# Two parts of every weight tile made by GpSimd DMAs (a casting load, a negation, an accumulating load) in place of a raw tile, ScalarE and VectorE

## The chip, the cores and the metric

The kernel runs on one core of one Trainium2 chip. The metric is device time in microseconds (us), first to last instruction of the program. Engines are PE (TensorE matmul), PEld (its weight load), DVE (VectorE), ACT (ScalarE), POOL (GpSimd) and SP (SyncE, which only issues DMAs here). Each works through its own list of instructions in order, and waits on semaphores for the others.

## The reference

A token sequence of 512 with 1024 features goes through two blocks. Block 1 is a mixer of four branches (Mamba-2, RG-LRU, retention, RWKV-7) and a feed-forward part; block 2 has two layers, each with three kinds of attention, a feed-forward part and a per-layer embedding. Nearly all arithmetic is in products of a normalised activation with a weight matrix, all in float32:

```python
def hybrid_mixer(h, w_in, ssm_p, lru_p, ret_p, rwkv_p, w_branch, w_out, cos, sin):
    proj = h @ w_in
    ...
    branch = jnp.einsum('bsmw,mwd->bsmd', ys, w_branch)
    ...
    return merged @ w_out

def conv_ffn(h, w_up, conv_w, conv_b, w_down):
    u = causal_dwconv(h @ w_up, conv_w, conv_b)
    val, gt = jnp.split(u, 2, axis=-1)
    return (jax.nn.silu(gt) * val) @ w_down
```

## The kernel before, in words

Activations stand with features on the 128 partitions and the 512 tokens along a row. To multiply float32 numbers at the fast rate, each operand is split in two parts that are exact in the rounded format F32R: `hi` is the operand rounded, `lo` is the operand minus `hi`. A product is three matmuls: hi by hi, lo by hi and hi by lo (`mm3`).

Weights come in tiles of 128 partitions by up to 1024 columns (512 KB), one tile for 128 output features and 1024 input features. `wtile` makes the two parts of one: SP loads the raw tile `wr` (3 buffers, `NWR`), ACT copies it rounded into `whi` (3 buffers), DVE writes the difference into `wlo` (2 buffers). A tile of 1024 columns then feeds 24 matmuls of 512 columns into one PSUM tile `pj`; a tile of 512 columns feeds 12, one of 256 columns 6. 579 such tiles go through the kernel. The third matmul of a tile is the first one that reads `wlo`.

A scheduler orders each engine's list when the program is built; the lists are fixed then. A tile's buffer is handed to the tile that comes as many tiles later as the pool has buffers, when the last matmul that reads it has ended. So `whi` of tile k can be written when PE has finished tile k-3, and `wlo` when PE has finished tile k-2.

Three places matter below. The feed-forward stretches (`ffn`, 1250 to 1640, 2250 to 2600 and 3280 to 3650 us) are 1024-column tiles back to back (768 columns at the end of each). In `attn_a_setup` (about 1640 to 1700 and 2640 to 2700 us) every projection tile alternates with a tile of `cmp_w1` that feeds only 8 matmuls of 256 columns. In `branch2` (to about 2160 and 3160 us) tiles of 512 columns of `w_br2` follow one another. POOL had little to do: zeroing of tiles, and the power -1/2 of each norm (`rsqrt`, the tiles `r`, `ors`, `rrs`).

Of the kernel before, what the change touches and what calls it, by code (L numbers as in the profile page):

```python
# [10 lines left out]
F32 = mybir.dt.float32  # L11
F32R = mybir.dt.float32r
I32 = mybir.dt.int32
AF = mybir.ActivationFunctionType
ALU = mybir.AluOpType
# [12 lines left out]
NWR = 3  # L28
# [10 lines left out]
def _param_layout():  # L39
    """Columns of the packed per-feature parameters: name -> (first column, columns)."""  # L40
# [17 lines left out]
# constants that depend on shapes alone: name -> (first column, columns)  # L58
# [15 lines left out]
class Unit:  # L74
    """Softmax attention of 128 queries over T sets of n keys that share a bank of scores."""
# [65 lines left out]
class B:  # L141
    """The parts of the program share these helpers, pools and constants."""
# [66 lines left out]
    def split(self, hi, lo, src, scale=None):  # L209
        """hi + lo == src (times a per-feature column), each part exact in the fast format."""  # L210
        if scale is None:
            self.act(hi, src, AF.Copy)
            self.tt(lo, src, hi.bitcast(F32), ALU.subtract)
        else:
            self.act(hi, src, AF.Copy, scale=scale)
            self.stt(lo, src, scale, hi.bitcast(F32), ALU.mult, ALU.subtract)

    def wtile(self, src, n=1024):
        raw = self.wr.tile([P, 1024], F32, tag="wr", name=self.name("wr"))
        self.dma(raw[:, :n], src)  # L220
        hi = self.wh.tile([P, 1024], F32R, tag="whi", name=self.name("whi"))
        lo = self.wh.tile([P, 1024], F32R, tag="wlo", name=self.name("wlo"), bufs=2)
        self.split(hi[:, :n], lo[:, :n], raw[:, :n])
        return hi, lo

    def mm3(self, out, ws, xs, first, last):
        """out += (wh + wl)^T (xh + xl) without the product of the two low parts."""
# [5 lines left out]
    def pmm(self, w, off, x, kc, m=P):  # L233
        """One chunk of m output features from the split weights w, from column off on."""
# [7 lines left out]
    def proj(self, src, x, kc=KC, m=P):  # L242
        """One chunk of m output features: src is [128, kc * m] of DRAM, x the split activations."""
        return self.pmm(self.wtile(src, kc * m), 0, x, kc, m)

    def rsqrt(self, out, ss, scale, eps):
        """out = (ss * scale + eps) ** -0.5 on a few columns."""
# [5 lines left out]
    def col_sums(self, out, xs):  # L253
        """out[:, t]: sums of the columns of all xs, tokens on partitions."""
# [6 lines left out]
    def rstd_rows(self, sq, dst, n=D):  # L261
        """sq: [128, S] (or several), whose column sums are sums of squares; dst[:, t] = rsqrt(mean + eps)."""
# [6 lines left out]
    def bcast_cols(self, r, dst):  # L269
        """The columns r [128, 4] of tokens as one row [., S] on every partition."""  # L270
# [9 lines left out]
    def softplus_neg_abs(self, out, ax, tmp):  # L280
        """out = log1p(exp(-ax)) for ax >= 0, by 2 atanh(e / (2 + e))."""
# [24 lines left out]
    def block1_consts(self):  # L306
# [23 lines left out]
        # 4 * softplus(-lam)  # L330
# [14 lines left out]
    def first_norm(self):  # L345
        """h = rms_norm(x) in two parts, features on partitions."""
# [28 lines left out]
    # -- RWKV --  # L375
    def rwkv_setup(self, pool):
# [11 lines left out]
        # w2: high parts on the lower half of the partitions, low parts on the upper; a2 the other way round  # L388
# [12 lines left out]
    def mix(self, pool, ps, ch, tag, bufs):  # L401
        """Token shift: x (1 - mu) + previous x mu."""
# [5 lines left out]
    def rwkv_lora(self, pool):  # L408
        """Chunks 24 (wl | al) and 25 (gl) of the mixed projection."""
# [20 lines left out]
    def lora(self, i, cs):  # L430
        """The second product of decay (0) or rate (1): (high + low) high, then high low."""
# [13 lines left out]
    def rwkv_core(self, pool, p):  # L445
# [6 lines left out]
        # decay  # L452
# [11 lines left out]
        # a  # L464
# [5 lines left out]
        # normalised key direction  # L470
# [19 lines left out]
        # bonus  # L490
# [6 lines left out]
        # values, tokens of a chunk on partitions, the two heads stacked  # L497
# [57 lines left out]
    def swap_halves(self, dst, src):  # L555
        """dst[(h, t), c, v] = src[(h, v), (c, t)] for halves h of the partitions and chunks c of 64."""
# [9 lines left out]
    def rwkv_inverse(self, pool):  # L566
        """(I + A)^-1 of every head and chunk, A strictly upper triangular: forward substitution in the two
        diagonal blocks of 32, one problem a partition, then the block above them by matrix products."""
# [25 lines left out]
        # four problems on the partitions: -X11 (A12 X22), with A12 and then (X11 A12)^T on block diagonals  # L594
# [60 lines left out]
    def rwkv_step(self, pool, p, c, st, ld, bank):  # L655
        """One chunk of the recurrence over the states of a pair of heads."""
# [32 lines left out]
    def rwkv_scan(self, pool, p, y):  # L689
        """The recurrence of a pair of heads, its norm and output."""  # L690
# [38 lines left out]
    # -- RG-LRU --  # L729
    def conv4(self, pool, ps, w, n, ch, b, tag, bufs=2, taps=4):  # L730
        """Causal depthwise convolution along the tokens of [128, S]."""
# [47 lines left out]
    # -- Mamba-2 --  # L779
    def silu_gate(self, pool, ps, tag, tmp, bufs=1):  # L780
        """silu(ps) = (1 + tanh(x / 2)) x / 2."""
# [7 lines left out]
    def ssm_setup(self, pool, tmp):  # L789
        """dt, its cumulative sums about each block's middle, and what follows from them."""  # L790
# [38 lines left out]
        # from the block's start, and about its middle  # L829
# [7 lines left out]
        # dt exp(end - cum)  # L837
# [112 lines left out]
    # -- retention --  # L950
    def rope(self, pool, ps, cos, sin, half, rows, tag, bufs=1, tmp=(("ropr", 1), ("rops", 1))):
        """x cos + swap(x) sin, halves of each head swapped across partitions by DMA."""
# [12 lines left out]
    def stack(self, pool, src, e, tag, bufs=1):  # L965
        """[high; low] parts of head e stacked on the partitions."""
# [6 lines left out]
    def dup(self, pool, src, e, tag, bufs=1):  # L973
        """The high part of head e on both halves of the partitions, and the low part."""
# [9 lines left out]
    def ret_pair(self, pool, j, y):  # L984
# [7 lines left out]
        # values with tokens on partitions  # L992
# [54 lines left out]
    def finish_ret(self):  # L1047
        """The last steps of the heads whose norms were begun one stage before."""
# [8 lines left out]
    # -- gates, branch products, merge --  # L1057
# [4 lines left out]
    def gates1(self, pool):  # L1062
        """tanh(gate / 2) of the four branches, chunk by chunk."""
# [7 lines left out]
    def branch(self, pool, m, y, gates, norm=None):  # L1071
        """merged (+)= (1 + tanh(gate / 2)) * (y_m W_m): twice the gated sum."""
# [20 lines left out]
    def norm_in(self, pool, c, x, w, acc, tag="nsq", bufs=2, gain=1.0):  # L1093
        """Chunk c of x (times gain) joins the sum of squares; its product with w is split into h."""
# [11 lines left out]
    def new_row(self):  # L1106
        """The row of 1 / rms by which products with h are still to be multiplied."""
# [6 lines left out]
    def out_proj(self, pool, w, m, xres, gain, g0, tag="xr", bufs=4, due=None):  # L1114
        """x += m w; the new x goes to DRAM, its normalised form to h. due: a row and gains still missing in x."""
# [15 lines left out]
    def ffn(self, up, down, conv, pool, done, mid=None, late=None):  # L1131
        """x + W_down (silu(gate) value); done(j, x_j) takes each finished chunk."""
# [51 lines left out]
    def embeddings(self, pool, i, tags=None):  # L1184
        """The per-layer embeddings p W of layer i, to DRAM."""
# [22 lines left out]
    def mid_norm(self, pool, fill):  # L1208
        """Block 1's last norm and block 2's first: x still lacks the first one's gain and row1, h the row of both."""
# [19 lines left out]
    def block1(self):  # L1229
# [10 lines left out]
        def weave(main, fill, ratio):  # L1240
            """One step of `fill` after every `ratio` steps of `main`; then what is left of fill."""
# [99 lines left out]
    def rope_tables(self, tmp):  # L1341
        """cos and signed sin of positions x frequencies, the angle reduced to [-pi, pi]."""
# [38 lines left out]
    def rope_load(self, pool, n, row):  # L1381
        """The rotary tables, times the row of 1 / rms if that is still due."""
# [18 lines left out]
    def rope2(self, pool, pt, cs, half, tag="ra", bufs=2):  # L1401
        """x cos + swap(x) sin, halves of each head swapped across partitions by DMA."""
# [16 lines left out]
    def to_tokens(self, pool, src, tag, rows=P, n=P, bufs=1):  # L1419
        """[rows, S] features x tokens to [128 tokens, 4, n]."""  # L1420
# [8 lines left out]
    def compress(self, pool, i, src, kv, out):  # L1429
        """gelu((blocks + pos) w1): leaves the hidden activations' transpose [128, 2, 64] in out."""  # L1430
# [15 lines left out]
        for t in range(4):  # L1446
            # high parts in columns 0 to 63 of each product's stationary operand, low parts in the others
# [659 lines left out]
```

## Time and profile before

| What | Value |
|---|---|
| Median of 3 runs | 3707.62 us (3706.73 to 3713.56) |
| Profiled execution, its own time as the span from first to last instruction | 3707.9 us |
| PE busy | 3630.3 us (98%) |
| DVE busy | 2328.7 us (63%) |
| ACT busy | 1543.6 us (42%) |
| POOL busy | 53.2 us (1%) |
| DMA queue q1 | 414.84 MB, 36.3% of 16 engines |

The profiled execution lies within 0.3 us of the median, so its rows can be added up against either. A share of busy time is a mean over stages; PE's 98% leaves 77.6 us in which it stood idle.

### The profile page before, as it was taken

What the parts mean: (1) busy time and instruction counts of PE and PEld (TensorE: products, weight loads), DVE (VectorE), ACT (ScalarE), POOL (GpSimd) and SP (SyncE); (2) the same over time, 40 slices, a digit from 0 to 9 for tenths busy, and PEclk for the clock granted to TensorE, in tenths of its full rate; (3) what the DMA queues carried; (4) which work ended last, traced back from release to release, by engine and by line L of the source; (5) the groups of instructions that cost most, each with busy time, mean ns of one, the idle gap of its engine ahead of it and who ended that gap; (6) DMA issues with size and microseconds to landing.
All of it is one profiled execution on the core that took longest, in us unless ns stands there. A gap on an engine that the chain in (4) does not pass through costs nothing.

```text
span 3707.9 us, 47402 instructions
## 1 busy us (share of the span) xinstructions
PE 3630.3 (98%) x17806; PEld 2953.0 (80%) x17806; DVE 2328.7 (63%) x4416; ACT 1543.6 (42%) x2619; POOL 53.2 (1%) x61
## 2 busy tenths in 40 slices
PE   8999999999999999999999999999999999999998
PEld 6887788877878788877888787888778887878886
DVE  6777897654454586657776655544677766554445
ACT  5665533323233353344555533222445655432223
POOL 0000000000000000000000000000000000000000
PEclk9999999999999999999999899999999999999999
DMA  5443545355543532344222124233442221343332
GB/s 182 141 135 116 154 123 142 107 152 161 158 132 108 162 108 91 103 135 150 76 66 68 58 82 154 92 96 95 139 134 80 64 69 55 102 141 96 95 93 97
DMA packets 230388, 417.86 MB, mean 113 GB/s; under 512 B 99632, under 2 KB 105648, under 8 KB 230032
## 3 DMA queue, kind: packets, MB, share of 16 engines
q1 hardware_dynamic: 230160, 414.84, 36.3%
q8 instruction: 141, 2.31, 0.3%
q14 instruction: 87, 0.71, 0.1%
HBM read 349.81 MB, written 55.38 MB: 109 GB/s over the span
## 4 chain that ended last, share of the span: by engine, by line
PE 66%; DVE 2%; ACT 1%; issue 0%; DMA 0%; POOL 0%; SPq 0%; POOLq 0%; DVEq 0%; ACTq 0%
PE pj L173 56%; PE ps L173 4%; PE pl L173 4%; PE ps L119 2%; DVE wlo L176 0%; DVE cc L176 0%; PE ps L1589 0%; POOL r L251 0%; ACT PT L166 0%; DVE ro L176 0%; ACT qf L166 0%; ACT P L167 0%; DVE kd L176 0%; DVE qf L176 0%; DVE xa L193 0%
## 5 line engine op out<-in xcount | busy, mean ns | idle before, releaser
L173 PE MATMUL pj<-hhi,whi 128*128 128x512 f32 (+1 forms) x2824 | 1137.6, 403 | 6.4 <-DVE scv L193 2.1
L173 PE MATMUL pj<-hhi,wlo 128*128 128x512 f32 (+1 forms) x2824 | 1127.2, 399 | 5.9 <-DVE wlo L176 5.8
L173 PE MATMUL pj<-hlo,whi 128*128 128x512 f32 (+1 forms) x2824 | 1128.0, 399 | 0.0
L166 ACT ACTIVATE whi<-wr 128x1024 fp32r<-128x1024 f32 (+3 forms) x579 | 573.4, 990 | 1289.1 <-PE pj L173 1140.3
L176 DVE TENSOR_TENSOR wlo<-wr,whi 128x1024 fp32r<-128x1024 f32 (+3 forms) x579 | 654.8, 1131 | 165.1 <-PE pj L173 104.2
L173 PEld LDWEIGHTS pj<-hhi,wlo 128*128 128x128 f32 (+1 forms) x2824 | 531.4, 188 | 135.9 <-DVE wlo L176 10.3
L173 PEld LDWEIGHTS pj<-hhi,whi 128*128 128x128 f32 (+1 forms) x2824 | 532.1, 188 | 130.8 <-issue 3.3
L173 PEld LDWEIGHTS pj<-hlo,whi 128*128 128x128 f32 (+1 forms) x2824 | 532.2, 188 | 122.8 <-issue 4.5
L173 PE MATMUL pj<-gl,whi 128*128 128x512 f32 x528 | 208.6, 395 | 0.0
L173 PE MATMUL pj<-gh,wlo 128*128 128x512 f32 x528 | 208.6, 395 | 0.0
L173 PE MATMUL pj<-gh,whi 128*128 128x512 f32 x528 | 208.5, 395 | 0.0
L176 DVE TENSOR_TENSOR fg<-pj,row 128x512 f32<-128x512 f32 x82 | 56.7, 691 | 212.7 <-PE pj L173 212.6
L176 DVE TENSOR_TENSOR xa<-pj,xa 128x512 f32<-128x512 f32 x72 | 49.8, 692 | 193.5 <-PE pj L173 193.3
L167 ACT ACTIVATE P<-ps,a 128x256 f32<-128x256 f32 (+3 forms) x256 | 128.3, 504 | 53.8 <-DVE a L189 49.9
L173 PE MATMUL pj<-o,whi 128*128 128x512 f32 x384 | 132.5, 421 | 0.0
L173 PE MATMUL pj<-yh,whi 128*128 128x512 f32 x320 | 131.1, 410 | 1.4 <-ACT yh L166 1.4
L173 PE MATMUL pj<-yl,whi 128*128 128x512 f32 x320 | 129.4, 404 | 0.5 <-DVE yl L176 0.5
L173 PE MATMUL pj<-yh,wlo 128*128 128x512 f32 x320 | 128.9, 403 | 0.0
L166 ACT ACTIVATE PT<-ps 128x256 f32<-128x256 f32 (+3 forms) x200 | 98.3, 492 | 71.0 <-PE ps L119 56.9
L173 PEld LDWEIGHTS pj<-gl,whi 128*128 128x128 f32 x528 | 99.0, 187 | 24.3
L173 PEld LDWEIGHTS pj<-gh,whi 128*128 128x128 f32 x528 | 99.0, 187 | 24.2
L173 PEld LDWEIGHTS pj<-gh,wlo 128*128 128x128 f32 x528 | 99.0, 187 | 24.2
(504 smaller groups left out, 5209.9 us busy)
## 6 DMA issues: line engine op xcount, KB each, us to landing
wr<-in_ffn_up SPq DMA_DIRECT2D x132, 512.0 KB, 3.4
wr<-in_w_in SPq DMA_DIRECT2D x122, 512.0 KB, 3.7
wr<-in_ffn_down SPq DMA_DIRECT2D x48, 512.0 KB, 3.5
wr<-in_w_bg SPq DMA_DIRECT2D x48, 512.0 KB, 3.4
wr<-in_w_gate SPq DMA_DIRECT2D x32, 512.0 KB, 3.5
wr<-in_w_branch SPq DMA_DIRECT2D x32, 512.0 KB, 3.5
wr<-in_w_out SPq DMA_DIRECT2D x24, 512.0 KB, 3.5
wr<-in_w_br SPq DMA_DIRECT2D x48, 256.0 KB, 2.6
```

The source lines that it names most:

```text
L119: b.nc.tensor.transpose(pt[:, k * P:(k + 1) * P], self.P[:, k * P:(k + 1) * P], b.ident)
L166: return self.nc.scalar.activation(out, in_, f, bias=bias, scale=scale)
L167: return self.nc.scalar.activation(out, in_, f, bias=bias, scale=scale, accum_out=accum)
L173: return self.nc.tensor.matmul(out, lhsT, rhs, start=start, stop=stop)
L176: return self.nc.vector.tensor_tensor(out, a, b, op=op)
```

## The change

`wtile` loses the raw tile. POOL issues a DMA that casts the weights from DRAM into `whi`, ACT writes the negative of `whi` into `wlo`, and POOL issues a second DMA of the same weights that adds to `wlo`. `whi` has 4 buffers in place of 3, `wlo` 3 in place of 2; the raw pool keeps one buffer for the two low-rank weight tiles that still use it. DVE no longer takes part, and SP no longer loads weights through `wtile`. The file also loses its comments, so that line numbers move by one to three.

```diff
-NWR = 3
+NWR = 1
+NWT = 4
...
     def wtile(self, src, n=1024):
-        raw = self.wr.tile([P, 1024], F32, tag="wr", name=self.name("wr"))
-        self.dma(raw[:, :n], src)
-        hi = self.wh.tile([P, 1024], F32R, tag="whi", name=self.name("whi"))
-        lo = self.wh.tile([P, 1024], F32R, tag="wlo", name=self.name("wlo"), bufs=2)
-        self.split(hi[:, :n], lo[:, :n], raw[:, :n])
+        hi = self.wh.tile([P, 1024], F32R, tag="whi", name=self.name("whi"), bufs=NWT)
+        lo = self.wh.tile([P, 1024], F32R, tag="wlo", name=self.name("wlo"), bufs=NWT - 1)
+        self.nc.gpsimd.dma_start(hi[:, :n], src)
+        self.act(lo[:, :n], hi[:, :n].bitcast(F32), AF.Copy, scale=-1.0)
+        self.nc.gpsimd.dma_start(lo[:, :n], src, accum_op=ALU.add)
         return hi, lo
```

The first place is the feed-forward part of block 2's first layer. On DVE of before, the two `wlo` of a pair of tiles stand between the products that take results out of PSUM (`fv`, `fg` from `pj`):

```order
L176 TENSOR_TENSOR fv4022_19737<-pj4021_19712,row3932_19302 128x512
L176 TENSOR_TENSOR wlo4031_19781<-wr4029_19778,whi4030_19780 128x1024
L176 TENSOR_TENSOR fg4027_19770<-pj4026_19745,row3932_19302 128x512
L176 TENSOR_TENSOR wlo4036_19814<-wr4034_19811,whi4035_19813 128x1024
L193 SCALAR_TENSOR_TENSOR fth4028_19772<-fth4028_19772,fg4027_19770 128x512
L176 TENSOR_TENSOR fth4028_19772<-fth4028_19772,fv4022_19737 128x512
L193 SCALAR_TENSOR_TENSOR gl3960_19343<-fth4028_19772,gh3952_19335 128x512
```

The list of POOL in the changed kernel at the same place has two DMAs a tile, and the cast of a tile stands ahead of the accumulation of the tile before it:

```order
L224 DMA whi3659_19225<-in_ffn_up2 128x1024
L226 DMA wlo3655_19188<-in_ffn_up2 128x1024
L224 DMA whi3663_19257<-in_ffn_up2 128x1024
L226 DMA wlo3660_19226<-in_ffn_up2 128x1024
L224 DMA whi3668_19295<-in_ffn_up2 128x1024
L226 DMA wlo3664_19258<-in_ffn_up2 128x1024
```

The list of ACT there has the negations where `whi` stood before, two to four tiles ahead of the result (`fth`, `gh`) that follows them:

```order
L167 ACTIVATE wlo3655_19188<-whi3654_19187 128x1024
L167 ACTIVATE wlo3660_19226<-whi3659_19225 128x1024
L167 ACTIVATE fth3649_19149<-fg3648_19147 128x512
L167 ACTIVATE gh3617_19000<-fth3649_19149 128x512
L167 ACTIVATE wlo3664_19258<-whi3663_19257 128x1024
L167 ACTIVATE wlo3669_19296<-whi3668_19295 128x1024
```

What moved: the writing of `wlo` from DVE's list to POOL's, with a step on ACT between its two DMAs; on DVE the rows of `wlo` are gone and nothing stands in their place.

The second place is `attn_a_setup` of the first layer, on POOL of the changed kernel (`in_cmp_w1` are the short tiles, `in_w_in2` the projections):

```order
L224 DMA whi2337_13406<-in_cmp_w1 128x1024
L226 DMA wlo2332_13364<-in_w_in2 128x1024
L224 DMA whi2339_13419<-in_w_in2 128x1024
L226 DMA wlo2338_13407<-in_cmp_w1 128x1024
L224 DMA whi2347_13468<-in_cmp_w1 128x1024
L224 DMA whi2349_13481<-in_w_in2 128x1024
L226 DMA wlo2340_13420<-in_w_in2 128x1024
L226 DMA wlo2348_13469<-in_cmp_w1 128x1024
L226 DMA wlo2350_13482<-in_w_in2 128x1024
```

Here two casts stand ahead of three accumulations at one point; on SP of before one load stood for each of these tiles.

The third place is the beginning, on POOL of the changed kernel (`in_w_pp` are the embeddings' weights, `r435` the first norm):

```order
L224 DMA whi25_125<-in_w_pp 128x1024
...
L226 DMA wlo26_126<-in_w_pp 128x1024
L224 DMA whi47_221<-in_w_pp 128x1024
L224 DMA whi57_382<-in_w_in 128x1024
L254 TENSOR_TENSOR r435_167<-rs36_168,mhalf_90 128x4
L224 DMA whi61_422<-in_w_in 128x1024
L226 DMA wlo48_222<-in_w_pp 128x1024
```

The accumulation into the second embedding tile (`wlo48`) now stands behind the first norm's power on POOL's list.

## Rows read from the trace of the kernel before

**Rows 1.** The page: busy us, share, instructions; then the chain that ended last.

```profile
PE 3630.3 (98%) x17806; PEld 2953.0 (80%) x17806; DVE 2328.7 (63%) x4416; ACT 1543.6 (42%) x2619; POOL 53.2 (1%) x61
PE 66%; DVE 2%; ACT 1%; issue 0%; DMA 0%; POOL 0%; SPq 0%; POOLq 0%; DVEq 0%; ACTq 0%
```

**Rows 2.** Waits of PE: for whom, total us, times, longest.

```profile
PE pj L173 <- ACT whi L166: 10.2, 3, 8.6
PE ps L173 <- DVE dg L176: 7.6, 10, 2.1
PE pj L173 <- DVE wlo L176: 5.8, 7, 1.5
...
PE ps L173 <- DVE hl L176: 5.4, 2, 3.6
```

**Rows 3.** Windows, feed-forward stretch: us, PE, PEld, DVE, ACT, POOL busy (instructions), PEclk, DMA share, GB/s.

```profile
3300.00:3400.00 100.00, 100.00 (x430) 80.60 (x429) 50.65 (x63) 29.21 (x36) 0.00 (x0) 1.00 0.30 95
```

**Rows 4.** Weight tiles' instructions in that stretch: duration ns least/median/most, first and last start.

```profile
L166 ACT ACTIVATE whi<-wr x18: 1062/1062/1062, 3299.7 to 3394.9; 128x1024 fp32r<-128x1024 f32 x18
L176 DVE TENSOR_TENSOR wlo<-wr,whi x18: 1218/1218/1218, 3300.5 to 3395.7; 128x1024 fp32r<-128x1024 f32 x18
```

**Rows 5.** DMA issues: count, KB each, median us from issue to landing.

```profile
wr<-in_ffn_up SPq DMA_DIRECT2D x132, 512.0 KB, 3.4
wr<-in_w_in SPq DMA_DIRECT2D x122, 512.0 KB, 3.7
wr<-in_w_pp SPq DMA_DIRECT2D x4, 512.0 KB, 4.5
xt<-in_xT SPq DMA_DIRECT2D x8, 256.0 KB, 6.0
```

**Rows 6.** POOL's instructions by line: count, busy us, mean ns, idle before.

```profile
L251 POOL TENSOR_TENSOR r<-rs,mhalf 128x4 f32<-128x4 f32 x15 | 16.2, 1078 | 2584.1 <-DVE rs L190 2584.1
L600 POOL MEMSET invbd<- 128x2048 f32 x1 | 1.8, 1814 | 57.1 <-DVE invt L176 57.1
```

**Rows 7.** Windows of weight tiles alone: DVE and ACT busy (tiles), PEclk, whole DMA share, GB/s.

```profile
800.00:900.00 100.00, 14.63 (x12) 13.74 (x13) 0.93 0.60 165
1600.00:1700.00 100.00, 21.13 (x20) 19.50 (x20) 0.98 0.51 160
2200.00:2300.00 100.00, 21.83 (x20) 19.27 (x19) 1.00 0.50 163
```

**Rows 8.** Timeline in `attn_a_setup`: start, us, engine, what, [idle before, releaser].

```profile
1677.87 0.50 PE L173 MATMUL pj<-hhi,wlo 128*128 128x512 f32 x1 [0.91 <-DVE wlo L176]
...
1685.03 0.39 PE L173 MATMUL ps<-whi,hl 128*128 128x256 f32 x1 [1.76 <-DVE hl L176]
1685.25 0.28 PE L173 MATMUL ps<-wlo,hl 128*128 128x256 f32 x1
1685.37 0.28 PE L173 MATMUL ps<-whi,hl 128*128 128x256 f32 x1
...
1686.31 0.63 PE L173 MATMUL pj<-hhi,whi 128*128 128x512 f32 x1
1686.74 0.63 PE L173 MATMUL pj<-hlo,whi 128*128 128x512 f32 x1
```

**Rows 9.** Windows: the stretch behind that wait, and the first full-rate loads.

```profile
1685.00:1690.00 5.00, 4.97 (x22) 4.32 (x23) 5.00 (x8) 1.91 (x3) 0.00 (x0) 0.66 0.48 124
8.00:14.00 6.00, 5.33 (x13) 3.79 (x14) 4.65 (x7) 5.05 (x9) 0.00 (x0) 1.00 1.00 385
```

**Rows 10.** Timeline of the beginning.

```profile
0.73 0.20 POOL masks.py:197 MEMSET ident<- 128x128 f32 x1 [0.29 <-POOLq L2098]
...
9.88 0.80 PE L173 MATMUL pj<-ph,wlo 128*128 128x512 f32 x1
...
17.52 1.02 POOL L251 TENSOR_TENSOR r<-rs,mhalf 128x4 f32<-128x4 f32 x1 [16.22 <-DVE rs L190]
...
19.89 0.80 PE L173 MATMUL pj<-ph,whi 128*128 128x512 f32 x1
```

## Prediction

> **What bounds the kernel now.** I read the page's busy line first. PE works 3630.3 of 3707.9 us [rows 1], so it stands idle for 77.6 us in all, and its own 66% is the main part of the chain that ended last. Then I read for whom PE waits. The longest waits are the 8.6 us before the first product, and a handful of 1 to 4 us for DVE; all waits for `wlo` come to 5.8 us [rows 2]. Then the feed-forward stretch: 430 products in 100 us, 0.233 us apart, at a granted clock of 1.00, while DVE is busy for half of the time and the DMA engines for 0.30 of it [rows 3]. 18 weight tiles go through it, one in 5.6 us, each with one copy of 1.06 us on ACT and one difference of 1.22 us on DVE [rows 4]. Nothing but PE is near its limit there.
>
> So the change can win only out of waits that are small already, and loses wherever a weight tile comes late. The question is how long the new way to a weight tile takes, against how early it can begin.
>
> **What is removed.** 579 differences leave DVE, some 655 us of its 2328.7 (1131 ns each as a mean over all sizes). They are hidden behind PE now, and DVE is not the bound, so most of that buys nothing. What it can buy is PE's waits for DVE: with `wlo` and `hl` gone it is 5.8 + 5.4 = 11.2 us; with `dg` too, 18.8 us; at the other end nothing, where those results wait for products anyway [rows 2]. I take **−11**. SP's weight loads go as well; SP's other loads can leave sooner, which no wait of PE in these rows asks for: 0. ACT keeps its 1.06 us a tile, as the negation.
>
> **What a tile's way becomes.** Before: a raw tile can be loaded three tiles ahead, and only one step of 1.2 us lies between the release of a `wlo` buffer and its next use. After: negation into the freed buffer, issue on POOL, landing of the accumulation, and then the first product that reads it.
> - Negation: 1.06 us, as the copy [rows 4].
> - Issue: the trace has no DMA on POOL. The nearest rows are its smallest work instruction, 1.08 us, and the memset of 1.81 us [rows 6]. Lower bound 0.6 (half of the first), upper 1.8; I take 1.08, the nearest.
> - Landing: a plain 512 KB load lands 3.4 to 3.7 us after its issue where the engines are calm [rows 5]. The accumulation moves the same weights, so 3.5 is the lower bound; twice that, 7.0, is the upper, if what is read of `wlo` counts in full. I take the middle, 5.25.
>
> Together 7.4 us, between 5.2 and 9.9.
>
> **What it has.** `wlo` has three buffers now, so the way of tile k begins when PE has finished tile k-3. Between that and the first use of `wlo` of tile k stand two tiles and two products, 50 in the feed-forward: 50 x 0.233 = 11.7 us. That hides 7.4 us, and even the upper end. The short places don't hide it. In `attn_a_setup` a projection alternates with eight products of 256 columns; these are 0.118 us apart when PE doesn't wait [rows 8], so the same stretch is 24 x 0.233 + 8 x 0.118 + 2 x 0.233 = 7.0 us. The 512-column tiles at the end of `branch2` give 26 x 0.233 = 6.1 us. I counted the products of the changed list for every tile: 36 tiles of 577 have less than 7.4 us, and what they lack adds up to 38 us; at 5.6 us it would be 9, at 9.1 us 119. Nearly all of it lies in the two `attn_a_setup` and the two `branch2`.
>
> To this comes POOL's order. An accumulation that waits for its negation holds the next cast back, and a late cast makes the next negation late. Going along POOL's list with 1.08 us an issue, 3.5 us for a cast and 5.25 for an accumulation, the shortages grow from 38 to about 62 us. With 3.5 for both they are 32, with 4 and 6 they are 93. I take **+62**.
>
> **Clock.** Behind a wait of 1.76 us the products of 512 columns stood 0.43 us apart instead of 0.233 [rows 8], and the granted clock of the next 5 us was 0.66 [rows 9]; that is about (1 − 0.66) x 5 = 1.7 us lost for a stall of that length. Of some 30 stalls I expect seven to be that long: **+12**, between 0 and 35.
>
> **Beginning.** POOL is ready from 0.9 us [rows 10]. Cast: issue 1.08, landing 4.5 as `w_pp` now [rows 5]; negation 1.06; issue 1.08; landing 4.5 again: the first `wlo` stands at about 13, and its first product runs at 9.88 now: +3. The engines are also full there, 1.00 at 385 GB/s [rows 9], with `xt` of 6.0 us among them. Then the accumulation into the second embedding tile stands on POOL behind the first norm's power, which waits until 17.5 us and takes 1.0; landed it is at about 25, and that tile's product chain begins at 19.9 [rows 10], so some +5. Together **+8**, between 4 and 12.
>
> **Sum**, on the profiled execution's 3707.9 us, which is 0.3 above the median: 3707.9 + 8 + 62 + 12 − 11 = **3779 us**. About 0.2%, 7.4 us, is what a measurement of this kernel can tell from no change.
>
> **Rivals.**
>
> *Two reads for an accumulation.* The sum treats the engines as free enough. In the feed-forward one pass over the weights costs 0.30 of them, and 0.30 is there already [rows 3]: with a cast and a plain accumulation 0.60, with an accumulation of two passes 0.90. Elsewhere I scale the pass by DVE's time on `wlo`: 800 to 900 us comes to 1.00 with two, 1600 to 1700 and 2200 to 2300 to 1.09 or 1.10 [rows 7]. In windows of 100 us over the whole span eight go beyond 1, by 42 us in all. 3779 + 42 = 3821, and with landings at the upper end up to 3900. For it: the old `wlo` has to come from somewhere. Against: windows with 0.60 run without a wait today.
>
> The Trainium skill, Collectives: The Full Stack, in Part 3, says that an adding transfer emits two source reads for each chunk where a copy emits one, so that a reduce-scatter runs at half the rate of an all-gather. By that rule this rival holds and the sum would be 3821. No trace here shows an adding transfer.
>
> *POOL or the DMA engines become the bound.* With three passes for an accumulation the feed-forward needs 1.20 of the engines, and 25 windows go over 1, by 561 us: 3707.9 + 561 + 8 = 4277. The same comes about if POOL needs more than 5.6 / 2 = 2.8 us for an issue, since each tile has two; at 3.5 us each it is 18 x 7.0 = 126 us for each of some 14 such stretches of 100. For it: POOL's smallest instruction takes 1.0 us for 4 elements a partition [rows 6], so it is not a quick engine. Against: that is still far from 2.8.
>
> *Hidden, no change.* If the way takes about 5.6 us, the shortages are 9 us by the buffers, and the start costs 4; the −11 cancels it: 3707.9 + 9 + 4 − 11 = 3710. For it: a third buffer, and 11.7 us in nine tenths of the kernel.
>
> *Faster.* The same short way, with a stall lengthening the cover of the two tiles behind it so that a third of the 9 us is paid, and DVE's 655 us freeing all 18.8 us of waits: 3707.9 + 3 + 4 − 18.8 = 3696. It is decided by the landing of an accumulation: it must be below about 3.5 us with an issue of about 1. Against: the waits in [rows 2] for `dg`, `hl` are short chains of one engine after another, of which `wlo` is only a part.
>
> **How the numbers follow.** Forecast, 3715 to 3810: 0.33. Two reads, 3810 to 3900: 0.17. Bound by POOL or the engines, above 3900: 0.18, half of it beyond 4000, since a part of a bound already costs 200 us. No change, 3700 to 3715: 0.15. Faster, below 3700: 0.17, of which two fifths are below 3692. The range 3692 to 4000 leaves out 0.07 and 0.11. Faster 0.17, same 0.15, slower 0.68. The forecast's own range is 3715 to 3810.
>
> **What the profile after would show.** For the price of a way: POOL's rows of DMAs (busy time each, 1.08 by the sum) and the landings of `whi` (3.5) and `wlo` (5.25). For the short places: PE waiting for a DMA into `wlo` or for the negation, some 30 times and about 60 us, nearly all within `attn_a_setup` and `branch2`, with a granted clock below 1 behind the long ones; none in the feed-forward. For the start: the first product with `wlo` at about 13 us. For the passes: a DMA share of 0.60 in 3300 to 3400 by the sum, 0.90 by two reads, 1.00 with PE below 430 products if the engines are the bound. DVE's busy time should fall to about 1675 us. I am wrong if PE waits in the feed-forward at all (a dearer issue or landing than my upper ends), or if `attn_a_setup` shows no waits for `wlo` (a cheaper one).

## The result, and the profile after

The changed kernel takes 3914.89 us (median of 4 runs, 3905.12 to 3920.14) against 3707.18 us beside it: ratio 1.0554, interval 1.0535 to 1.0573. The profiled execution spans 3917.8 us, 210 us more than the one of before. The forecast was 3779.

The page, as [rows 1]: busy time of each engine; the DMA queues (packets, MB, share of 16 engines); the chain that ended last.

```profile
PE 3698.1 (94%) x17806; PEld 2993.5 (76%) x17806; DVE 1765.3 (45%) x3837; ACT 1533.2 (39%) x2619; POOL 872.6 (22%) x1219
...
q0 software_dynamic: 166752, 558.05, 67.6%
q1 hardware_dynamic: 146784, 135.82, 11.9%
...
PE 53%; issue 24%; DMA 10%; POOL 8%; DVE 3%; ACT 2%; SPq 0%; POOLq 0%; DVEq 0%; ACTq 0%
```

The bytes on POOL's queue are the weights twice, once for each DMA, but the engines' time went from 36.3% of 3707.9 us (1346 us) to 79.5% of 3917.8 (3115 us). PE's idle time went from 77.6 to 219.7 us (+142), and the same 17806 products took 68 us longer; 142 + 68 is the whole difference. Whom PE waits for, as [rows 2]:

```profile
PE pj L174 <- DMA wlo<-in_w_in: 29.4, 14, 5.8
PE ps L174 <- DVE acc L177: 25.8, 8, 6.6
PE pj L174 <- DVE xr L177: 11.1, 8, 2.1
PE pj L174 <- DMA wlo<-in_w_pp: 11.0, 3, 9.9
PE ps L174 <- DMA wlo<-in_cmp_w: 9.7, 5, 3.4
...
PE pj L174 <- DMA whi<-in_w_pp: 9.0, 1, 9.0
PE ps L174 <- DMA zb_kr<-s_KR: 8.7, 2, 6.9
```

Adding up all such rows by what they wait for: weights 86.5 us (16.9 before), everything else 123.0 us (51.2 before). The second sum is the one to look at: `acc`, `xr` and `zb_kr` are no weight tiles, and before the change PE waited 4.8 us for `acc` and never for `xr`.

Windows, as [rows 3] and [rows 7]: a feed-forward stretch, and the two that hold the first `attn_a_setup`. Columns: PE, PEld, DVE, ACT, POOL busy; PEclk; DMA share; GB/s.

```profile
3600.00:3700.00 100.00, 100.00 (x430) 80.49 (x429) 24.91 (x36) 26.02 (x30) 25.39 (x36) 1.00 0.91 188
...
1700.00:1800.00 100.00, 85.43 (x338) 66.50 (x337) 37.32 (x67) 39.23 (x59) 25.98 (x39) 0.90 0.90 225
1800.00:1900.00 100.00, 87.58 (x405) 69.50 (x404) 42.68 (x97) 36.94 (x59) 22.66 (x32) 0.88 0.80 176
```

In the feed-forward the DMA engines stand at 0.91 and PE still gets its 430 products. DMA issues, as [rows 5], and POOL's own time for them, as [rows 6] (busy us, mean ns):

```profile
whi<-in_ffn_up POOLq DMA_DIRECT2D x132, 512.0 KB, 4.4
wlo<-in_ffn_up POOLq DMA_DIRECT2D x132, 512.0 KB, 6.3
...
wlo<-in_w_in POOLq DMA_DIRECT2D x122, 512.0 KB, 6.6
...
rb<-ro SPq DMA_DIRECT2D x96, 64.0 KB, 5.1
...
xr<-xs SPq DMA_DIRECT2D x16, 256.0 KB, 5.5
```

```profile
L224 POOL DMA_DIRECT2D whi<-in_ffn_up x132 | 73.7, 558 | 426.8 <-PE pj L174 413.2
L226 POOL DMA_DIRECT2D wlo<-in_ffn_up x132 | 113.2, 857 | 143.4 <-ACT wlo L167 138.0
```

Not only the weights are later: a 64 KB load of `rb` lands in 5.1 us, an `xr` in 5.5. The same two rows before:

```profile
rb<-ro SPq DMA_DIRECT2D x96, 64.0 KB, 2.0
...
xr<-xs SPq DMA_DIRECT2D x16, 256.0 KB, 2.8
```

DVE waits 269.7 us for DMAs, 27.4 before. What that does to PE is seen at the norm at the end of the first layer's `branch2`. SP's queue, then DVE:

```profile
2362.72 0.38 SPq L171 DMA_DIRECT2D xr<-xs  x1
```

```profile
2371.80 0.75 DVE L194 SCALAR_TENSOR_TENSOR xr<-xr,pars,csr 128x512 f32<-128x512 f32 x1 [7.45 <-DMA xr<-xs]
2372.66 0.69 DVE L177 TENSOR_TENSOR xr<-pj,xr 128x512 f32<-128x512 f32 x1
```

The next residual tile is 9.1 us on its way; the result in `pj` can only then be taken out of PSUM, and PE waits for `xr` and, at the end of the norm, for `acc`. The same load before:

```profile
2225.03 0.75 DVE L193 SCALAR_TENSOR_TENSOR xr<-xr,pars,csr 128x512 f32<-128x512 f32 x1 [2.23 <-DMA xr<-xs]
```

A stall for weights looks like this (`attn_a_setup`; POOL, then PE):

```profile
1768.31 0.87 POOL L226 DMA_DIRECT2D wlo<-in_w_in  x1 [2.24 <-ACT wlo L167]
1771.12 0.54 POOL L224 DMA_DIRECT2D whi<-in_w_in  x1 [1.94 <-PE pj L174]
...
1777.34 0.79 PE L174 MATMUL pj<-hhi,wlo 128*128 128x512 f32 x1 [5.82 <-DMA wlo<-in_w_in]
```

From issue to use 9.0 us. Both executions run almost the same list of products on PE, so the starts of products with the same number can be set against each other; the difference is the loss up to there:

| Product | Place | Starts before, after (us) | Lost so far (us) |
|---|---|---|---|
| 800 | after the beginning | 179, 193 | 14 |
| 3200 | block 1, branches | 638, 680 | 42 |
| 6400 | norm behind block 1's branches | 1279, 1363 | 83 |
| 8000 | norm behind block 1's feed-forward | 1652, 1745 | 93 |
| 8800 | first `attn_a_setup` done | 1813, 1943 | 129 |
| 11200 | norm behind the first `branch2` done | 2277, 2429 | 151 |
| 12400 | feed-forward | 2557, 2709 | 151 |
| 13600 | second `attn_a_setup` done | 2817, 2995 | 178 |
| 16400 | norm behind the second `branch2` done | 3363, 3569 | 206 |

Inside the feed-forwards nothing is lost (products 6800 to 7900 stay 89 us behind, 11200 to 12400 151); the 10 us between products 6400 and 8000 lie at the two ends of block 1's, around the norms. Block 1's branches with the norm behind them, where the forecast put next to nothing, lose 69 us.

### The profile page after: what moved, and what is told of

The parts are those of the page before. It is cut to its first block, busy times and chain, and to the rows that moved or that the text cites. A ratio compares the mean times of both kernels' runs of the same rounds, so it can differ in the third digit from the quotient of the medians.

```text
span 3917.8 us, 48081 instructions
## 1 busy us (share of the span) xinstructions
PE 3698.1 (94%) x17806; PEld 2993.5 (76%) x17806; DVE 1765.3 (45%) x3837; ACT 1533.2 (39%) x2619; POOL 872.6 (22%) x1219
## 3 DMA queue, kind: packets, MB, share of 16 engines
q0 software_dynamic: 166752, 558.05, 67.6%
## 4 chain that ended last, share of the span: by engine, by line
PE 53%; issue 24%; DMA 10%; POOL 8%; DVE 3%; ACT 2%; SPq 0%; POOLq 0%; DVEq 0%; ACTq 0%
PE pj L174 40%; PE ps L174 7%; POOL wlo L226 4%; PE pl L174 4%; POOL whi L224 3%; DMA xr<-xs 2%; DMA wlo<-in_w_in 1%; PE ps L120 1%; DMA yraw<-y 1%; DMA rb<-ro 1%; DMA srow<-d_mid 1%; DMA xr<-in_xT 1%; ACT wlo L167 1%; DMA xs<-e 0%; DMA whi<-in_w_in 0%
## 5 line engine op out<-in xcount | busy, mean ns | idle before, releaser
L174 PE MATMUL pj<-hhi,wlo 128*128 128x512 f32 (+1 forms) x2824 | 1142.6, 405 | 35.1 <-DMA wlo<-in_w_in 29.4
L174 PE MATMUL pj<-hhi,whi 128*128 128x512 f32 (+1 forms) x2824 | 1152.9, 408 | 4.7 <-issue 1.8
L174 PE MATMUL pj<-hlo,whi 128*128 128x512 f32 (+1 forms) x2824 | 1139.7, 404 | 0.3 <-DVE hlo L194 0.3
L167 ACT ACTIVATE wlo<-whi 128x1024 fp32r<-128x1024 f32 (+3 forms) x579 | 572.1, 988 | 1156.5 <-PE pj L174 957.3
L174 PEld LDWEIGHTS pj<-hhi,wlo 128*128 128x128 f32 (+1 forms) x2824 | 540.1, 191 | 169.5 <-DMA wlo<-in_w_in 34.6
L174 PEld LDWEIGHTS pj<-hhi,whi 128*128 128x128 f32 (+1 forms) x2824 | 540.5, 191 | 133.7 <-issue 9.3
L224 POOL DMA_DIRECT2D whi<-in_w_in x122 | 71.3, 588 | 481.9 <-PE pj L174 474.3
L224 POOL DMA_DIRECT2D whi<-in_ffn_up x132 | 73.7, 558 | 426.8 <-PE pj L174 413.2
L226 POOL DMA_DIRECT2D wlo<-in_w_in x122 | 106.3, 872 | 245.4 <-ACT wlo L167 222.6
L226 POOL DMA_DIRECT2D wlo<-in_ffn_up x132 | 113.2, 857 | 143.4 <-ACT wlo L167 138.0
```

The source lines that it names most:

```text
L167: return self.nc.scalar.activation(out, in_, f, bias=bias, scale=scale)
L174: return self.nc.tensor.matmul(out, lhsT, rhs, start=start, stop=stop)
L224: self.nc.gpsimd.dma_start(hi[:, :n], src)
L226: self.nc.gpsimd.dma_start(lo[:, :n], src, accum_op=ALU.add)
```

## The experiments

**Theory A**: the adding DMA costs the engines about two passes, and the traffic makes transfers land late, those of the weights and all others. **Theory B**: the longer way of a tile through POOL's and ACT's lists costs the time, whatever the bytes. All ratios are against the kernel before on the same chip. "Engines' time" is the two queues' share times the span; the last two columns are PE's idle time and busy time over those of before.

| Run | Median us | Ratio, interval | Engines' time us | Idle + | Busy + |
|---|---|---|---|---|---|
| the change | 3914.89 | 1.0554, 1.0535 to 1.0573 | 3115 | 142 | 68 |
| e1 plain second | 3799.15 | 1.0254, 1.0235 to 1.0272 | 2424 | 74 | 24 |
| e2 traffic on before | 3834.36 | 1.0357, 1.0336 to 1.0378 | 2827 | 78 | 46 |
| e3 cast alone | 3767.69 | 1.0166, 1.0143 to 1.0190 | 2321 | 42 | 18 |
| e4 accumulate alone | 3891.35 | 1.0498, 1.0475 to 1.0522 | 2986 | 130 | 50 |
| e5 narrow second | 3712.29 | 1.0022, 1.0011 to 1.0032 | 1690 | 13 | −7 |
| e6 one more lo | 4081.19 | 1.1015, 1.0989 to 1.1041 | 3041 | 260 | 108 |
| e7 negation on DVE | 3916.34 | 1.0583, 1.0549 to 1.0616 | 3092 | 145 | 66 |
| e8 before, three lo | 3700.23 | 0.9984, 0.9975 to 0.9994 | 1351 | 0 | −8 |
| e9 one more hi | 3860.98 | 1.0415, 1.0394 to 1.0436 | 3081 | 117 | 37 |
| e10 e6, narrow | 3814.24 | 1.0296, 1.0279 to 1.0312 | 1666 | 85 | 20 |
| e11 cast, no raw | 3726.09 | 1.0057, 1.0040 to 1.0074 | 1450 | 17 | 3 |

**e1, the second DMA without adding.**

```diff
-        self.nc.gpsimd.dma_start(lo[:, :n], src, accum_op=ALU.add)
+        self.nc.gpsimd.dma_start(lo[:, :n], src)
```

> The changed kernel with the second DMA of each tile writing the rounded weights over the negation in place of adding to it (so lo holds the rounded weights, not the difference; every instruction, buffer and wait stays). Theory A, the adding DMA reads twice and its traffic makes every transfer late: DMA share in the feed-forward 0.60 in place of 0.91, landing of the second DMA about 4.4 us in place of 6.3, the 64 KB loads rb<-ro about 3 us in place of 5.1; PE's waits for weights fall from 86 us to about 40 and its other waits from 123 to about 85; some 3780 us. Theory B, the longer way through POOL's and ACT's lists costs the time whatever the bytes: waits for weights stay above 70 us, others above 105, and the time stays above 3860 us.

Its landings and its feed-forward window:

```profile
whi<-in_ffn_up POOLq DMA_DIRECT2D x132, 512.0 KB, 3.8
wlo<-in_ffn_up POOLq DMA_DIRECT2D x132, 512.0 KB, 4.7
...
rb<-ro SPq DMA_DIRECT2D x96, 64.0 KB, 4.7
```

```profile
3500.00:3600.00 100.00, 100.00 (x430) 80.24 (x430) 22.83 (x33) 24.61 (x28) 18.82 (x36) 1.00 0.65 189
```

The second DMA lands 1.6 us sooner and the share falls from 0.91 to 0.65: the adding, at the same bytes, is what fills the engines from 0.65 to 0.91. By the ratios it costs 3.0% of the time, 111 us of the 208. PE waits 50 us for weights and 92 us for others, the latter a little above A's 85. The time is 19 us above A's figure and far below B's. `rb`, at 4.7 us, did not come back as A had it.

**e2, more traffic on the kernel before**, two plain copies of each raw tile to memory:

```diff
         self.split(hi[:, :n], lo[:, :n], raw[:, :n])
+        for j in range(2):
+            dum = self.dr.tile([P, 1024], F32, tag=f"dum{j}", name=self.name("dum"), bufs=4)
+            self.nc.gpsimd.dma_start(dum[:, :n], raw[:, :n])
```

> The kernel before with two more copies of each raw weight tile by POOL's DMAs into memory that nobody reads; the way of the weights stays as before. Theory A: DMA share in the feed-forward about 0.90, the ordinary loads as late as in the changed kernel (rb<-ro about 5 us, xs<-e about 5.5), PE's waits that are not for weights about 110 us against 68, and with the clock lost behind them some 3780 us. Theory B: about 3708 us, within 15.

```profile
3500.00:3600.00 100.00, 100.00 (x430) 80.50 (x429) 47.44 (x58) 27.24 (x33) 19.03 (x36) 1.00 0.82 288
```

Nothing of the change's way is in this kernel, and it loses 128 us. PE's waits that are not for weights come to 103 us (A: 110), and `xs` lands in 5.7 us as A had it, but `rb` in 3.6 in place of about 5, the share is 0.82 in place of 0.90, and A's time was too low by 54 us. Nor is it traffic alone: a copy reads `wr` and so holds the raw buffer, and SP, whose list runs in order, waits for that.

```profile
SPq L170 <- DMA dum<-wr: 297.6, 168, 9.4
```

Part of the 128 us can come from these held buffers, in the weights (42 us of waits, where 16.9 stood) and in the small loads behind them on SP's list; how much wasn't tested. The change has no such hold, so e2 supports theory A without settling it. e1 and e5 are the cleaner tests.

**e3, the cast alone**, and **e4, the accumulation alone.**

```diff
 e3, from the kernel before
-        self.split(hi[:, :n], lo[:, :n], raw[:, :n])
+        self.nc.gpsimd.dma_start(hi[:, :n], src)
+        self.tt(lo[:, :n], raw[:, :n], hi[:, :n].bitcast(F32), ALU.subtract)
 e4, from the kernel before, NWR = 2, three lo buffers
-        self.split(hi[:, :n], lo[:, :n], raw[:, :n])
+        self.act(hi[:, :n], raw[:, :n], AF.Copy)
+        self.ts(lo[:, :n], hi[:, :n].bitcast(F32), -1.0)
+        self.nc.gpsimd.dma_start(lo[:, :n], src, accum_op=ALU.add)
```

> The kernel before with hi by the casting DMA; the raw tile is still loaded by SP and DVE still takes the difference. Two passes: share 0.60 in the feed-forward. Theory A: ordinary loads about 1 us later, time +10 to +35, so 3717 to 3743 us. Theory B: DVE's difference now waits for a cast that is issued when PE has left tile k-3, and DVE's other work behind it: +40 or more, above 3748 us.

> The kernel before with hi copied by ACT from a raw tile loaded by SP (2 raw buffers), the negation on DVE and lo by the adding DMA (3 lo buffers): no cast on POOL. Three passes again: share about 0.90. Theory A: ordinary loads as late as in the changed kernel, PE's waits that are not for weights above 100 us, time 3820 to 3900 us. Theory B: nothing on POOL holds an accumulation back any more, so the weights' waits fall below 40 us and the time below 3790 us.

They give the price of each kind of pass. POOL's queue in e3 (579 casts), then in e4 (579 accumulations):

```profile
q0 software_dynamic: 83376, 279.02, 26.3%
```

```profile
q0 software_dynamic: 83376, 279.02, 42.8%
```

That is 26.3% of 3768.5 = 991 us of the 16 engines for the casts, and 42.8% of 3888.2 = 1664 us for the accumulations, of the same packets and bytes: 1.7 times as much. SP's plain loads before took 1346 − 466 = 880 us (466 is what q1 still has after the change), so an accumulation is worth 1.9 plain loads. 991 + 1664 = 2655 us is what q0 of the changed kernel shows (67.6% of 3917.8 = 2648).

As tests they hit less well. e3 lost 61 us, which is B's figure; e11 below takes it apart. e4's 3891 is within A's range, and B's is missed by 100 us; but A wanted above 100 us of PE's waits for others, and there were 75; for weights PE waited 121 us. There a tile's copy, negation and accumulation all begin with the release of tile k-3; that this is why was not tested.

**e5, the same lists without the bytes.**

```diff
-        self.nc.gpsimd.dma_start(lo[:, :n], src, accum_op=ALU.add)
+        self.nc.gpsimd.dma_start(lo[:, :64], src[:, :64], accum_op=ALU.add)
```

> The changed kernel with the adding DMA cut to the first 64 of each tile's columns (the rest of lo stays the negated hi, so the sum is not the reference's); every instruction, buffer and wait stays. DMA share in the feed-forward about 0.35. Theory A, traffic: the ordinary loads are back within 0.5 us of before, PE's waits that are not for weights at about 55 us as before, time 3712 to 3740 us, what is left being the beginning and the longer way. Theory B, the way through POOL and ACT: still above 3760 us.

```profile
PE 3623.7 (98%) x17806; PEld 2951.2 (79%) x17806; DVE 1765.8 (48%) x3837; ACT 1533.6 (41%) x2619; POOL 873.6 (24%) x1219
...
wlo<-in_ffn_up POOLq DMA_DIRECT2D x132, 32.0 KB, 3.1
```

1.0022: two DMAs a tile on POOL (still 874 us busy), the negation and every wait of the change stay, and 201 of the 208 us are gone. B, as the whole cause, falls. PE's waits that are not for weights are back at 57 us, and those for weights at 24. Taken with e1, the change's 5.5% (205 us by the ratio) divides into 8 us for the lists, 86 for the bytes of a second pass that doesn't add, and 111 for the adding. What e5 can't separate: its second DMA also lands sooner itself, in 3.1 us in place of 6.3. A wrong point of A: `rb` still takes 4.0 us and `xr` 4.2 us from issue to landing, and DVE still waits 155 us for DMAs, without cost to PE. The landing of a small load alone thus says little. SP no longer stands behind weight loads (2293 us of waiting for `wlo` before, 26 after), so its loads now leave in groups; that this makes them land later is likely, and wasn't tested.

**e7, the negation on DVE.**

```diff
-        self.act(lo[:, :n], hi[:, :n].bitcast(F32), AF.Copy, scale=-1.0)
+        self.ts(lo[:, :n], hi[:, :n].bitcast(F32), -1.0)
```

> The changed kernel with the negation on DVE in place of ACT. If ACT, held by negations that wait for late casts, keeps its other results from PE, PE's waits for ACT (35 us against 19 before) go back to 20 and the time falls by 15 to 40 us, to 3875 to 3900 us. If transfers are late whoever negates, it stays within 12 us of 3915.

3916.34: no gain. PE's waits for ACT fell to 22 us as the first theory had it, and its waits for DVE rose from 76 to 85 and for weights to 91. Which of the two engines negates makes no difference to the time here.

**e6 and e9, one more buffer in block 2**, for `lo` or for `hi` (the raw pool was moved into block 1 to make room; `wx` is a pool of one buffer, and `wk` counts the tiles of block 2):

```diff
 e6
...
+        pool, nb = (self.wx, 1) if self.wx is not None and self.wk % 4 == 0 else (self.wh, NWT - 1)
+        lo = pool.tile([P, 1024], F32R, tag="wlo", name=self.name("wlo"), bufs=nb)
 e9
...
+        pool, nb = (self.wx, 1) if self.wx is not None and self.wk % 5 == 0 else (self.wh, NWT)
+        hi = pool.tile([P, 1024], F32R, tag="whi", name=self.name("whi"), bufs=nb)
```

> The changed kernel with a fourth buffer for lo in block 2 only (the raw buffer moved into block 1 to make room). If the short places lack time because lo has too few buffers, PE's waits for weights in the two attn_a_setup, about 40 us in sum, halve, and with the clock behind them the kernel takes 3860 to 3890 us; block 1 stays 88 us behind the kernel before. If the waits there come from casts and accumulations being served late by POOL and the DMA engines in any case, it stays within 12 us of 3915.

e6 was some 165 us slower than the change. All of that is in block 2 (product 8800 starts no later than in the change), much of it in the feed-forwards: PE now waits 73 us for `wlo` there. Neither theory had that. POOL in the second feed-forward, e6:

```profile
3719.95 0.87 POOL L229 DMA_DIRECT2D wlo<-in_ffn_up  x1 [7.01 <-ACT wlo L167]
...
3724.08 0.89 POOL L227 DMA_DIRECT2D whi<-in_ffn_up  x1
3731.62 0.85 POOL L229 DMA_DIRECT2D wlo<-in_ffn_up  x1 [6.64 <-ACT wlo L167]
```

and the changed kernel:

```profile
3623.58 0.55 POOL L224 DMA_DIRECT2D whi<-in_ffn_up  x1 [3.42 <-PE pj L174]
3624.90 0.85 POOL L226 DMA_DIRECT2D wlo<-in_ffn_up  x1 [0.77 <-ACT wlo L167]
3629.18 0.55 POOL L224 DMA_DIRECT2D whi<-in_ffn_up  x1 [3.42 <-PE pj L174]
```

The reading: with as many buffers for `lo` as for `hi`, both of a tile come free at once, and the scheduler puts a tile's accumulation on POOL ahead of the next tile's cast. POOL then waits for a negation that waits for a cast, and the next cast can't leave. With one `hi` more, the cast of the next tile stands ahead. e9 and e10 test that:

> The changed kernel with the spare buffer of block 2 given to hi (5) in place of lo (3): on POOL two casts now stand ahead of the accumulation of an older tile. If e6 was slow because POOL's list there puts an accumulation, which waits for its negation, ahead of the next cast, this order undoes that: PE waits for no weight in the feed-forward parts, and the kernel takes 3885 to 3920 us, some 160 below e6. If a fourth weight buffer in block 2 does harm as such (more transfers at a time), it is above 3980 us too.

> e6 with the adding DMA cut to 64 columns, as in e5 (lo keeps the negated hi elsewhere). Order theory: the cast lands in 3.8 us, the negation takes 1.06, the two issues 1.4, in sum 6.3 us for a tile against PE's 5.6, so the feed-forward parts of block 2 still lose some 0.7 us a tile wherever the two stand one behind the other: 3740 to 3830 us. If e6 was slow by traffic alone: 3700 to 3725 us as e5.

e9: 3860.98, 220 us below e6 for the same buffer spent on `hi`, and about 1.4% below the change (1.0415 against 1.0554), below the 3885 to 3920 us that were expected; PE's waits for ACT and weights both fell by 11 us. e10, the slow order without the traffic, lost 102 us against e5. Its POOL, second feed-forward of block 2, and a window there:

```profile
3645.83 0.86 POOL L229 DMA_DIRECT2D wlo<-in_ffn_up  x1 [4.80 <-ACT wlo L167]
...
3652.12 0.85 POOL L229 DMA_DIRECT2D wlo<-in_ffn_down  x1 [4.88 <-ACT wlo L167]
...
3658.48 0.86 POOL L229 DMA_DIRECT2D wlo<-in_ffn_down  x1 [4.95 <-ACT wlo L167]
```

```profile
3550.00:3650.00 100.00, 92.34 (x381) 71.61 (x380) 18.04 (x27) 21.16 (x24) 22.71 (x32) 0.98 0.36 90
```

One tile in 6.3 us, as worked out, against PE's 5.6, and 381 products in place of 430 with the engines at 0.36. So a bad order on POOL alone cost 102 us, about as much as the adding (111 us); the change has the better order, and the traffic costs it the time.

e10 also says how far a sum of waits can be trusted. PE's waits that are not for weights come to 110 us in it, at that share of 0.36. The largest of them is

```profile
PE pj L174 <- DVE fv L177: 31.2, 27, 2.4
```

and in the feed-forward a late cast stands behind it. On ACT:

```profile
3650.77 1.06 ACT L167 ACTIVATE wlo<-whi 128x1024 fp32r<-128x1024 f32 x1 [5.24 <-DMA whi<-in_ffn_down]
3651.74 0.61 ACT L167 ACTIVATE fth<-fg 128x512 f32<-128x512 f32 x1
```

The result `fth` comes after a negation that waits for that cast, and DVE's products, which free `pj`, wait for `fth` (35 us in 3550 to 3650). A late weight tile can thus show as a wait for a result.

**e11, e3 without the raw load**:

```diff
 from e3
-        raw = self.wr.tile([P, 1024], F32, tag="wr", name=self.name("wr"))
-        self.dma(raw[:, :n], src)
-        self.tt(lo[:, :n], raw[:, :n], hi[:, :n].bitcast(F32), ALU.subtract)
+        self.tt(lo[:, :n], hi[:, :n].bitcast(F32), hi[:, :n].bitcast(F32), ALU.subtract)
```

> e3 without the raw load: the cast into hi stays, DVE writes hi minus hi (zeros, with the same duration) into lo, so lo's weights are left out. One pass in all, as before the change, with e3's way from the freed hi buffer over the cast to DVE. If e3's 61 us came from the second pass, this is within 15 us of the kernel before. If they came from the way (the cast can only start when PE has left tile k-3, and DVE's difference waits for it), it keeps 40 us or more: above 3745 us.

1.0057: 21 us, between the two figures, so neither theory has e3's 61 us alone: some 40 go with the second pass and 21 are left with the way.

**e8, the kernel before with its buffers as 2 raw and 3 lo.**

```diff
-NWR = 3
+NWR = 2
-        lo = self.wh.tile([P, 1024], F32R, tag="wlo", name=self.name("wlo"), bufs=2)
+        lo = self.wh.tile([P, 1024], F32R, tag="wlo", name=self.name("wlo"), bufs=3)
```

> The kernel before with 2 raw buffers and 3 lo buffers. PE's waits for lo and hi of 16.9 us fall by at most a third: 3700 to 3708 us; if the third raw buffer was needed, 3710 to 3725 us.

3700.23 over 10 runs, 0.9984 (0.9975 to 0.9994): the only version here below both kernels, by 5 to 6 us. PE's waits didn't shrink (67.8 us in sum, 68.1 before); the products ran 8 us shorter in sum, in one profiled execution of each. Why is open.

## Why the prediction was right or wrong

It had the direction and the feed-forward, where PE waits for weights 0.6 us in all. It forecast 71 us where 208 came: 3915 lies inside the wide range of 3692 to 4000 and 105 us above the forecast's own, 3715 to 3810. It falls where the chances had *POOL or the DMA engines become the bound*, but not by that rival's mechanism: an accumulation costs about two passes and not three, and POOL holds 0.86 us for an issue and not 2.8. The terms of its sum against what was measured:

| Term | Forecast us | Measured us |
|---|---|---|
| Beginning | +8 | +14 |
| Weights late, short places and POOL's order | +62 | +59 (67.3 without the 19.2 of the beginning's tiles, against 8.3) |
| PE's waits for the rest | −11 | +72 (123.0 against 51.2) |
| Clock (slower products) | +12 | +68 |

The beginning is the loss at product 800 and holds some of the waits of the rows below it, so the rows overlap by a few us; idle and busy time, 142 + 68, close exactly.

**The step that failed** is "The sum treats the engines as free enough", together with "SP's other loads can leave sooner, which no wait of PE in these rows asks for: 0". The engines' time was weighed in windows of 100 us against 1.00, and the feed-forward shows that 0.91 is indeed bearable where the work can be done ahead. But a transfer that lies in a chain, out to memory and back within a norm or a scan, comes late at once, as the `xr` of 9.1 us did. The −11 for freed waits became +72, and block 1's branches, with no term at all, lost 69 us. e5 shows the +72 gone when the traffic goes (57 us of such waits, where 51 stood before the change). It also shows what the −11 was worth: in e5 the waits that it named, for DVE's `wlo`, `hl` and `dg`, fell from 19.7 to 8.2 us, but others grew, and in sum PE waited 81 us where 68 stood. How the 72 us divide between small loads that come late and casts that come late and hold a negation, with the results behind it, is open; e7 took 13 us from PE's waits for ACT and gained no time.

**The clock term was mis-sized.** The price used, 1.7 us for a stall of 1.8 us, was read from [rows 8, 9], and seven such stalls were counted. With 210 us of waits in place of 68, the products took 68 us more: the mean granted clock was 0.90 and 0.88 in the two windows with `attn_a_setup`. Over the nine runs that lost more than 40 us of idle time, each us of it came with 0.2 to 0.6 us of slower products (e10 20 for 85, e2 46 for 78). A share of all idle time would have been the better term than a count of long stalls, though these runs leave it wide.

**The price of an accumulation** was the rival's, not the sum's. The share in the feed-forward is 0.91, as *two reads* had it (0.90; 0.60 by the sum), and an accumulation costs the engines 1.9 plain loads. The Trainium skill (Collectives: The Full Stack, Part 3) says of a collective's add that it needs two source reads for each chunk where a copy needs one; the 1.9 agrees with it. The rival's time of 3821, up to 3900, was still too low, for the reason above. That the engines as a whole don't bound the kernel was right: e6 is slower than the change with less of their time (3041 us). It isn't shown for every stretch: in four windows of the changed kernel the share is 0.94 to 0.97 (0.97 in 1300 to 1400, with 375 products), and whether the engines are the bound there for a while was not tested.

**The way of a tile** was priced within its bounds: issue 0.86 (1.08 was taken) and 0.56 for a cast; landing 6.3 to 6.6 (5.25 was taken, bounds 3.5 and 7.0), together 8.2 to 8.5 us for 7.4. That +62 met +59 so well is luck. The prediction's own walk along POOL's list gave 93 us with landings of 4 and 6, and 4.4 to 4.8 and 6.3 to 6.6 were measured, at shorter issues; by it, more than 62 was due. The place was half right too: the two `attn_a_setup` have 41 us, but `branch2`, which was to have most of the rest, has 3 (`w_br` and `w_bg`), and weights behind it (`w_out`, 6.7) and in block 1 (`w_rv`, 9.2) appear instead.

**The beginning**: 13 us was forecast for the first `wlo`, and it was there at 20.9. Its accumulation left POOL only at 10.93, behind a cast that landed at 9, and took 10 us beside the loads of the inputs, where the sum had 4.5:

```profile
10.93 0.91 POOL L226 DMA_DIRECT2D wlo<-in_w_pp  x1 [8.50 <-ACT wlo L167]
...
20.91 0.80 PE L174 MATMUL pj<-ph,wlo 128*128 128x512 f32 x1 [9.87 <-DMA wlo<-in_w_pp]
```

**Two readings were off** without weight for the time. PE's waits for `wlo` were 6.7 us, not 5.8 ([rows 2] leaves out a row of 0.9 for `ps`). And DVE's busy time fell to 1765 us, not to 1675: neighbouring instructions on DVE overlap in the trace, so the 579 differences last 655 us in sum but cover less time.

What stays open is how the 111 us of the adding divide between its own late landing and the lateness that it causes: from e1 to the change PE's waits for weights rose by 36 us, its other waits by 31, and the products by 44. e9 shows that in block 2 one `hi` buffer more, which lets casts leave earlier, wins back about 54 us at the same traffic, so part of what is called traffic here is paid only because a cast leaves late.

## What to carry to other kernels

A transfer that takes work off an idle engine isn't free because the queues have room on average: look for the transfers that lie in a chain (out and back within a norm or a scan), and ask what each will take when the engines are at 0.9. Price an adding DMA as two passes (1.9 here). Where one in-order queue issues both halves of a tile, look at the order that the scheduler gives it: here the half that starts the chain needed one buffer more than the half that ends it, or the second half stood in front of the next tile's first. And don't read a wait by its name alone: a late weight tile can show as a wait for a result.

## What the runs showed of the hardware that was not expected

- An accumulating DMA of 512 KB costs the 16 engines 1.7 times a casting one and 1.9 times a plain load, at the same packets, and holds POOL 0.86 us against 0.56 for the casts beside it (0.53 for either DMA in e1, where none adds).
- A DMA cut to 64 of 1024 columns holds POOL as long (0.86 us), and the engines' time for 579 of them still shows: 1690 us in all against some 1457 for casts and the rest.
- One buffer more made a kernel some 165 us slower, by the order that it gave to POOL's list; the same buffer spent on the other half made it 54 us faster.
